# Keeping both halves of the spread conditioning vectors in SBUF, with Silu taken once on a DRAM copy

## The chip, the cores and the metric

One core of one Trainium2 chip runs the whole program. The metric is the device time of one execution in microseconds (us); lower is better. The engines are PE (TensorE), DVE (VectorE), ACT (ScalarE), POOL (GpSimd) and SP, which in this kernel issues every DMA. Each engine works through its own list of instructions strictly in order.

## The reference, cut to what matters

Two layers of a diffusion backbone on 256 latent and 256 context tokens, width 2048, everything in float32.

```python
sc, sc_ctx = silu(c), silu(c_ctx)                        # two vectors of 2048
for l in range(2):
    shift, scale, gate = split(sc @ w_ada[l] + b_ada[l], 3)
    shift_c, scale_c, gate_c = split(sc_ctx @ w_ada[l] + b_ada[l], 3)
    h_lat = rms_norm(x, norm_g[l]) * (1 + scale) + shift
    h_ctx = rms_norm(xc, norm_g[l]) * (1 + scale_c) + shift_c
    # projections of h by w_in[l]; attention of two kinds of heads; SiLU gates -> y
    x  = x + gate * (y_lat @ w_out[l])
    if l == 0:
        xc = xc + gate_c * (y_ctx @ w_out[l])
return rms_norm(x, final_g)
```

The products with `w_ada` are matrix times vector: 2 x 2048 x 6144 weights, for one or two vectors.

## The kernel before, in words

**Matmuls.** Every large product is done in three passes of a split: `wtile` (L105) loads a 512 KB tile of weights (`raw`, four slots, or at the start also `rad`, two slots), ACT copies it to `hi` (L114), DVE or, for each fifth tile, POOL forms `lo = raw - hi` (L116), and `mm3` (L138) issues three matmuls (L141 to L143). Results go to four PSUM banks `acc`, which DVE or ACT must empty (`evac_into`, L453 to L457) before PE can reuse them.

**Conditioning.** The shift and scale of layer 0 come from PE at the start (`ada_pe`, loads `ra`, L210, matmuls L229). The rest, gate of layer 0, shift, scale and gate of layer 1, is a background task (`ada_rest`, L296; one step of it is pulled in by `wtile` at a rate set by `bg_rate`). A step of `ada_half` (L252) loads a 512 KB tile `rad` of the transposed weights and lets DVE multiply and sum it with a half of `c`, spread over all partitions in the tile `cb` (L273, output `junk`, sum in `as`). With two vectors a step has four such instructions, here called **junk** instructions; there are 448 in all, on 128 `rad` tiles. `rad` has two slots, so a load waits until the junk instructions of the tile before last are done.

**The tile `cb`.** One slot (L250). Its first user is not the background task but the accumulator `q0` of the first query projection (L875), which holds it until the start of the first attention. `ada_rest` then goes through half 0, 1, 1, 0, 0, 1 of the vectors, and each call of `ada_half` takes a new `cb`, loads 1 MB into it by a broadcast DMA from DRAM (L259) and has ACT take Silu in place (L260). That makes six loads, six Silus and the changes between ACT's function tables that they bring, as attention uses Exp.

**Order.** A scheduler (`schedule_with_timeline_sim`) sets the order of each engine's list when the program is built, with the program's order as priority. So a change in what waits for what can move instructions far from the edit.

Layer 0 runs: first projections in seven parts while `w_ada` streams in (0 to 200 us); the last part of the projections `kv`, `q0`, `g0`, `q1` (`rest`, L925); attention of the first head group, for two blocks of heads (`gqa_heads`); projections `cq`, `ckv`, gates; the second group of heads (`mla_pair`, `mla_heads`); the output projection (`out_steps`, L773). Layer 1 follows in the same way.

## Time and profile before

| | us |
|---|---|
| median of three runs | 1416.0 (1414.63 to 1416.56) |
| the profiled execution | 1413.77 |
| its span (first to last instruction) | 1412.0 |
| PE busy | 1331.6 (94%) |
| DVE busy | 1094.0 (77%) |
| ACT busy | 602.6 (43%) |
| POOL busy | 404.0 (29%) |
| mean granted clock of PE | 0.984 of full speed |

The profile is one execution. Busy time is the sum of an engine's instructions; a view by stretches tells for each stretch how long each engine was busy, the clock that PE was granted (1.00 is 2.4 GHz, 0.50 is 1.2 GHz, and between them a mix of the two levels) and the share of the DMA engines in use. A row of waits names who waited for whom, with the total, the count and the longest. A row of the timeline has the start, the duration, the engine, the line, the operation, output<-input, and in brackets how long the engine was idle before it and what ended the wait.

### The profile page before, as it was taken

Reading aid. Unit: us, or ns where it says so; the run is one execution under the profiler, and the core shown is the slowest. Engines: PE = TensorE matmul, PEld = TensorE weight load, DVE = VectorE, ACT = ScalarE, POOL = GpSimd, SP = SyncE. Lnnn points to the kernel's source line nnn. Section 1 sums busy time; section 2 is a strip of 40 time slices with the busy share of each in tenths; the row PEclk is TensorE's granted clock in tenths of the full one; section 3 lists DMA queues with packets and bytes.
Section 4 is the critical chain, followed back from the end, with each engine's and each line's share of the span. In section 5 each row is a group of like instructions: output and inputs, shape, how many; then the busy total and the mean of one; then the engine's idle time right before and its main releaser. Section 6 shows DMA issues by size and latency. Waiting matters only on the chain.

```text
span 1412.0 us, 21026 instructions
## 1 busy us (share of the span) xinstructions
PE 1331.6 (94%) x7516; PEld 1128.1 (80%) x7516; DVE 1094.0 (77%) x2297; ACT 602.6 (43%) x974; POOL 404.0 (29%) x385
## 2 busy tenths in 40 slices
PE   5999999999997999898998999999999999999996
PEld 4776787877786987787886778898898989888884
DVE  2776548998887998989998965976787776857566
ACT  4322224535443242455532134665555644454443
POOL 0110015423223130221222213533234431223335
PEclk9999999999999999999999999999999999999999
DMA  9987733455554766443576665655775757733444
GB/s 310 354 276 268 271 104 104 135 164 181 160 187 155 209 217 199 148 147 120 179 247 210 209 214 178 202 161 169 237 257 162 237 156 259 257 108 124 157 139 144
DMA packets 142120, 272.47 MB, mean 193 GB/s; under 512 B 8336, under 2 KB 53824, under 8 KB 140608
## 3 DMA queue, kind: packets, MB, share of 16 engines
q1 hardware_dynamic: 142016, 271.13, 59.5%
q8 instruction: 59, 0.97, 0.3%
q14 instruction: 45, 0.37, 0.1%
HBM read 264.78 MB, written 6.32 MB: 192 GB/s over the span
## 4 chain that ended last, share of the span: by engine, by line
PE 55%; DVE 21%; DMA 11%; issue 6%; ACT 3%; POOL 2%; SPq 1%; DVEq 0%; POOLq 0%; ACTq 0%
PE acc L143 16%; PE acc L141 16%; PE acc L142 15%; DVE junk L273 8%; DMA rad<-in_w_adaT 7%; DVE lo L116 5%; PE att L592 3%; PE att L229 2%; PE att L615 1%; DMA raw<-in_w_in 1%; DMA cb<-in_cr 1%; DVE sm L597 1%; DVE pt L148 1%; DMA ra<-in_w_ada 1%; ACT hi L114 1%
## 5 line engine op out<-in xcount | busy, mean ns | idle before, releaser
L114 ACT CAST hi<-raw 128x1024 fp32r<-128x1024 f32 (+2 forms) x279 | 271.9, 977 | 380.1 <-PE acc L142 206.4
L116 DVE TENSOR_TENSOR lo<-raw,hi 128x512 fp32r<-128x512 f32 (+2 forms) x446 | 307.5, 731 | 88.8 <-PE acc L143 39.5
L116 POOL TENSOR_TENSOR lo<-raw,hi 128x512 fp32r<-128x512 f32 (+2 forms) x112 | 153.4, 1390 | 466.1 <-PE acc L143 317.4
L141 PE MATMUL acc<-hi,h 128*128 128x512 f32 (+1 forms) x672 | 239.3, 359 | 7.4 <-ACT cq L455 4.8
L142 PE MATMUL acc<-hi,h 128*128 128x512 f32 (+1 forms) x672 | 237.7, 356 | 0.0
L273 DVE CUSTOM_DVE_ANT_0 junk<-rad,cb 128x512 bf16<-128x512 f32 x224 | 175.0, 781 | 76.0 <-DMA rad<-in_w_adaT 50.4
L143 PE MATMUL acc<-lo,h 128*128 128x512 f32 (+1 forms) x672 | 227.4, 359 | 2.7 <-DVE lo L116 2.4
L273 DVE CUSTOM_DVE_ANT_0 junk<-rad,cb,as 128x512 bf16<-128x512 f32 x224 | 193.1, 862 | 3.8
L142 PE MATMUL acc<-h,lo 128*128 128x512 f32 (+1 forms) x512 | 171.4, 340 | 2.5 <-DVE lo L116 2.5
L143 PE MATMUL acc<-h,hi 128*128 128x512 f32 (+1 forms) x512 | 170.0, 338 | 0.0
L603 POOL TENSOR_SCALAR p<-p,sm 128x512 f32<-128x512 f32 (+1 forms) x96 | 85.8, 900 | 283.9 <-DVE sm L601 247.9
L141 PE MATMUL acc<-h,hi 128*128 128x512 f32 (+1 forms) x512 | 165.0, 341 | 0.3 <-ACT q L455 0.3
L143 PE MATMUL acc<-lo,y 128*128 128x512 f32 x384 | 146.3, 400 | 9.2 <-DVE lo L116 8.1
L141 PE MATMUL acc<-hi,y 128*128 128x512 f32 x384 | 150.7, 398 | 2.4 <-ACT y L147 2.0
L142 PE MATMUL acc<-hi,y 128*128 128x512 f32 x384 | 151.9, 396 | 0.2 <-DVE y L148 0.2
L141 PEld LDWEIGHTS acc<-hi,h 128*128 128x128 f32 x672 | 127.2, 189 | 28.9 <-ACT cq L455 5.0
L143 PEld LDWEIGHTS acc<-lo,h 128*128 128x128 f32 x672 | 124.6, 189 | 22.3 <-DVE lo L116 4.1
L142 PEld LDWEIGHTS acc<-hi,h 128*128 128x128 f32 x672 | 127.0, 189 | 15.5
L142 PEld LDWEIGHTS acc<-h,lo 128*128 128x128 f32 x512 | 96.8, 190 | 12.8 <-DVE lo L116 3.6
L143 PEld LDWEIGHTS acc<-h,hi 128*128 128x128 f32 x512 | 96.7, 190 | 9.8
L141 PEld LDWEIGHTS acc<-h,hi 128*128 128x128 f32 x512 | 93.6, 190 | 13.0 <-issue 2.5
L143 PEld LDWEIGHTS acc<-lo,y 128*128 128x128 f32 x384 | 73.4, 192 | 28.0 <-DVE lo L116 12.2
(219 smaller groups left out, 2281.4 us busy)
## 6 DMA issues: line engine op xcount, KB each, us to landing
rad<-in_w_adaT SPq DMA_DIRECT2D x128, 512.0 KB, 4.5
raw<-in_w_in SPq DMA_DIRECT2D x125, 512.0 KB, 4.5
raw<-in_w_out SPq DMA_DIRECT2D x72, 512.0 KB, 4.0
ra<-in_w_ada SPq DMA_DIRECT2D x32, 1024.0 KB, 8.4
raw<-in_w_in SPq DMA_DIRECT2D x48, 288.0 KB, 3.1
raw<-in_w_ukv SPq DMA_DIRECT2D x16, 512.0 KB, 3.5
cb<-in_cr SPq DMA_DIRECT2D x6, 1024.0 KB, 7.2
raw<-in_w_uq SPq DMA_DIRECT2D x12, 512.0 KB, 3.7
```

What stands on the lines that cost most here:

```text
L114: nc.scalar.copy(h, t)
L116: e.tensor_tensor(out=lo[:, c], in0=t[:, c], in1=fr(h[:, c]), op=ALU.subtract)
L141: mm(out, lhsT=ah, rhs=bh, start=first, stop=False)
L142: mm(out, lhsT=al, rhs=bh, start=False, stop=False)
L143: return mm(out, lhsT=ah, rhs=bl, start=False, stop=last)
L148: self.nc.vector.tensor_tensor(out=lo, in0=src, in1=fr(hi), op=ALU.subtract)
L229: nc.tensor.matmul(ps[32 * g : 32 * g + 32, :], lhsT=self.scp[:, m + i, o : o + 32], rhs=rs[kind, m][:, i, :], start=run is runs[0] and j ...
L273: nc.vector.tensor_tensor_reduce(out=junk, in0=r[:, cs], in1=cb[:, v, cs], scale=1.0, scalar=o if i else 0.0, op0=ALU.mult, op1=ALU.add, a ...
L592: self.order = nc.tensor.matmul(banks[j], lhsT=q[:, qs], rhs=k[:, ks], start=i == 0, stop=i == len(score) - 1)
L597: nc.vector.tensor_reduce(out=nb[:, c], in_=v, axis=AX.X, op=ALU.max)
L603: nc.gpsimd.tensor_scalar(out=pr[j], in0=pr[j], scalar1=l[:, j : j + 1], scalar2=1.0, op0=ALU.mult, op1=ALU.mult)
L615: nc.tensor.transpose(b[:, k, j * P : (j + 1) * P], pr[j][:, (i + k) * P : (i + k + 1) * P], self.ident)
```

## The change

The broadcast source becomes a small DRAM tensor `sc_d`. A new function `spread_c`, called in `layer0` after the third part of the first projections, loads both vectors as 32 rows of 128 into a temporary tile, takes Silu of them on ACT, and writes them to `sc_d`. The tile `cb` gets two slots, and `ada_half` keeps the tile of each half in a dictionary: the first call with half 0 loads it, the first call with half 1 loads the other, and the four later calls use what is there. Silu on the spread tile is gone. The scratch for DMA descriptors is set to 2 KB when the program is created.

```diff
+    def spread_c(self):
+        nc = self.nc
+        cr = self.tmp("cr")[: 2 * KT, :P]
+        nc.sync.dma_start(out=cr, in_=self.a["cr"].rearrange("v (k p) -> (v k) p", p=P))
+        nc.scalar.activation(cr, cr, AF.Silu)
+        self.sc_d = self.dp.tile([2, D], F32, name="sc_d")
+        nc.sync.dma_start(out=self.sc_d.rearrange("v (k p) -> (v k) p", p=P), in_=cr)
...
     def cb_tile(self):
-        return self.tp.tile([P, 2, 1024], F32, tag="cb", name=self.nm("cb"), bufs=1)
+        return self.tp.tile([P, 2, 1024], F32, tag="cb", name=self.nm("cb"), bufs=2)
...
     def ada_half(self, half, work):
-        cb = self.cb_tile()
         hs = slice(half * 1024, half * 1024 + 1024)
-        with self.behind():
-            nc.sync.dma_start(out=cb, in_=self.a["cr"][:, hs].partition_broadcast(P))
-        nc.scalar.activation(cb, cb, AF.Silu)
+        if half not in self.cb:
+            self.cb[half] = self.cb_tile()
+            with self.behind():
+                nc.sync.dma_start(out=self.cb[half], in_=self.sc_d[:, hs].partition_broadcast(P))
+        cb = self.cb[half]
...
                 modulated(nxt)
+            if p[0] == 2:
+                self.spread_c()
         self.start = False
...
-    nc = bacc.Bacc("TRN2", target_bir_lowering=False, num_devices=1)
+    nc = bacc.Bacc("TRN2", target_bir_lowering=False, num_devices=1, dynamic_dma_scratch_size=2048)
```

The edit makes the changed file longer: its L283 is L273 of the kernel before, L463 is L453, L465 is L455, L219 is L210, L329 is L319.

The order of the lists changes at three places. The first is **SP's list in the first projections**, behind the loads of the third part. Before (`cs` is a table for the rotary positions, `ra` weights of `ada_pe`):

```order
L96 DMA raw_812<-in_w_in 128x2x512
L486 DMA cs_798<-in_rope 128x512
L210 DMA ra_820<-in_w_ada 128x8x256
L210 DMA ra_822<-in_w_ada 128x8x256
L210 DMA ra_840<-in_w_ada 128x8x256
L210 DMA ra_842<-in_w_ada 128x8x256
```

After:

```order
L96 DMA raw_817<-in_w_in 128x2x512
L178 DMA cr_798<-in_cr 32x128
L496 DMA cs_803<-in_rope 128x512
L181 DMA sc_d<-cr_798 32x128
L219 DMA ra_825<-in_w_ada 128x8x256
L219 DMA ra_827<-in_w_ada 128x8x256
L219 DMA ra_845<-in_w_ada 128x8x256
L219 DMA ra_847<-in_w_ada 128x8x256
```

Four loads of `ra` now stand behind a write that waits for ACT's Silu.

The second is **DVE's list where the background task begins**. Before, it begins in the first attention, behind the first softmax (`q_55` is the accumulator of `q1`):

```order
L598 SCALAR_TENSOR_TENSOR sm_2096<-sm_2096,scq_810 128x2
L273 ISA junk_1651,as_1647<-rad_1649,cb_1644 128x512
L273 ISA as_1647 128x1
L453 TENSOR_TENSOR q_55_354<-acc_2469,q_55_354 128x512
L453 TENSOR_TENSOR q_55_354<-acc_2476,q_55_354 128x512
```

After, it begins behind the modulation of the last part, among the evacuations of `q0` (named `cb_326`) and `q1`:

```order
L375 SCALAR_TENSOR_TENSOR h_1405<-xT_100,mod_87,h_1404 128x256 x8
L283 ISA junk_1655,as_1651<-rad_1653,cb_1649 128x512
L283 ISA as_1651 128x1
L463 TENSOR_TENSOR cb_326<-acc_1437,cb_326 128x512
...
L116 TENSOR_TENSOR lo_1577<-rad_1574,hi_1576 128x512 x2
L283 ISA junk_1700,as_1651<-rad_1698,cb_1649 128x512
L283 ISA as_1651 128x1
L463 TENSOR_TENSOR q_55_354<-acc_1507,q_55_354 128x512
L463 TENSOR_TENSOR q_55_354<-acc_1514,q_55_354 128x512
```

The background task has moved ahead by the whole end of the projections. Counted in the two lists, the junk instructions that stand ahead of four points on DVE are: the last `qT` of the second block of heads, 51 before and 96 after; the first `kn` of the second head group, 230 and 283; that group's last maximum (L597), 316 and 365; the twelfth product with the gate in the output projection (L810), 392 and 392. From there on the counts agree.

The third is **ACT's list at the projection `cq`**. Before:

```order
L114 CAST hi_4165<-raw_4163 128x576
L260 ACT_TABLE_LOAD
L260 ACTIVATE cb_3746<-cb_3746 128x2048
L319 ACTIVATE junk_4035,sm_4034<-cq_3682 128x512
L455 COPY cq_3682<-acc_3709 128x512
L319 ACTIVATE junk_4056,sm_4055<-cq_3682 128x512
```

After:

```order
L114 CAST hi_4165<-raw_4163 128x576
L465 COPY cq_3685<-acc_3712 128x512
L329 ACTIVATE junk_4035,sm_4034<-cq_3685 128x512
L329 ACTIVATE junk_4056,sm_4055<-cq_3685 128x512
L114 CAST hi_4216<-raw_4214 128x576
```

The Silu of `cb` and its table load no longer stand ahead of the evacuation of `cq`. Over the whole list of ACT the table loads fall from 22 to 14, and SP's list has two loads of `cb` in place of six.

## Rows read from the trace of the kernel before

**Rows 1.** Stretches by stage: us, busy time (count) by engine, PE clock, DMA share, GB/s

```profile
176.00:243.00 67.00, 65.49 (x300) 53.82 (x299) 44.65 (x78) 21.72 (x32) 25.80 (x30) 1.00 0.31 95
243.00:329.00 86.00, 80.56 (x416) 67.65 (x415) 81.67 (x195) 39.09 (x69) 34.24 (x32) 0.96 0.51 160
329.00:577.00 248.00, 230.50 (x1230) 198.22 (x1229) 217.53 (x530) 91.80 (x145) 60.14 (x58) 0.98 0.59 186
577.00:731.00 154.00, 147.35 (x876) 128.76 (x875) 142.70 (x350) 77.23 (x145) 33.83 (x37) 0.99 0.49 157
731.00:857.00 126.00, 117.54 (x504) 94.44 (x503) 100.24 (x213) 34.59 (x51) 30.53 (x22) 0.96 0.65 213
857.00:1234.00 377.00, 367.39 (x2292) 329.75 (x2291) 285.05 (x527) 200.19 (x304) 138.55 (x130) 1.00 0.66 210
```

**Rows 2.** Waits of the whole run, total us, count, longest

```profile
DVE junk L273 <- DMA rad<-in_w_adaT: 50.4, 39, 4.2
DVE junk L273 <- ACT cb L260: 23.4, 5, 7.9
```

**Rows 3.** DVE's waits from 329 to 577 us

```profile
DVE junk L273 <- ACT cb L260: 13.2, 2, 7.9
DVE junk L273 <- DMA rad<-in_w_adaT: 10.4, 12, 2.0
```

**Rows 4.** DVE's longest wait from 577 to 731 us

```profile
DVE junk L273 <- ACT cb L260: 4.2, 1, 4.2
```

**Rows 5.** Timeline of ACT, then of PE, at the third load of `cb`

```profile
444.19 1.28 ACT L260 ACT_TABLE_LOAD   x1 [7.68 <-DMA cb<-in_cr]
445.48 1.91 ACT L260 ACTIVATE cb<-cb 128x2048 f32<-128x2048 f32 x1
...
448.53 0.61 PE L141 MATMUL acc<-hi,h 128*128 128x288 f32 x1 [4.77 <-ACT cq L455]
```

**Rows 6.** Stretch around it

```profile
436.00:460.00 24.00, 17.54 (x91) 15.38 (x91) 15.43 (x34) 11.03 (x20) 11.26 (x12) 0.86 0.44 145
```

**Rows 7.** Timeline of SP in the first projections

```profile
58.52 0.65 SPq L486 DMA_DIRECT2D cs<-in_rope  x1
60.72 0.37 SPq L210 DMA_DIRECT2D ra<-in_w_ada  x1
...
71.79 3.38 SPq L96 DMA_DIRECT2D raw<-in_w_in  x1
```

**Rows 8.** DMA issues from 55 to 90 us: size, median us to landing

```profile
ra<-in_w_ada SPq DMA_DIRECT2D x6, 1024.0 KB, 10.2
cs<-in_rope SPq DMA_DIRECT2D x1, 256.0 KB, 10.4
```

**Rows 9.** Chain of waits, the matmuls that use those `ra`

```profile
82.03 1.86 PE att L229 x32
```

**Rows 10.** Junk instructions from 176 to 329 us: busy us, mean ns, idle before

```profile
L273 DVE CUSTOM_DVE_ANT_0 junk<-rad,cb,as 128x512 bf16<-128x512 f32 x25 | 22.3, 891 | 0.3
L273 DVE CUSTOM_DVE_ANT_0 junk<-rad,cb 128x512 bf16<-128x512 f32 x26 | 19.9, 765 | 0.7 <-DMA rad<-in_w_adaT 0.6
```

**Rows 11.** Timeline of POOL, then of DVE, near 430 us

```profile
430.68 3.46 POOL L116 TENSOR_TENSOR lo<-raw,hi 128x512 fp32r<-128x512 f32 x2 [24.47 <-PE acc L143]
...
430.61 0.69 DVE L273 CUSTOM_DVE_ANT_0 junk<-rad,cb 128x512 bf16<-128x512 f32 x1
431.22 0.09 DVE L273 DVE_READ_ACCUMULATOR2_ANT as<- 128x1 f32 x1
431.34 1.65 DVE L273 CUSTOM_DVE_ANT_0 junk<-rad,cb,as 128x512 bf16<-128x512 f32 x1
```

**Rows 12.** Timeline of DVE, then of SP, near 186 us

```profile
185.66 1.29 DVE L116 TENSOR_TENSOR lo<-rad,hi 128x512 fp32r<-128x512 f32 x2 [4.85 <-PE acc L143]
186.88 1.28 DVE L453 TENSOR_TENSOR q<-acc,q 128x512 f32<-128x512 f32 x2
...
187.02 0.34 SPq L96 DMA_DIRECT2D rad<-in_w_adaT  x1
```

More of the change, by code (lines that the diff above doesn't have):

```diff
@@ L61, in __init__ @@
         self.bg = []
-        self.sums, self.ada_l1 = {}, False
+        self.sums, self.ada_l1, self.cb = {}, False, {}
         self.bg_rate = 0.0
```

## The prediction

> **What bounds the kernel now.** I read the stretches by stage first [rows 1]. PE is busy in 92 to 98% of every stage, so PE's work is the floor and only its idle time and its clock can be won. What a stage loses is its width minus PE's busy time, plus its width times what the clock lacks to 1.00 (while the clock is at its lower level a matmul takes twice as long). From 176 to 857 us that is 39.6 us of idle (1.5, 5.4, 17.5, 6.7 and 8.5 in the order of the rows) and 15.0 us of clock (0, 3.4, 5.0, 1.5, 5.0).
>
> The reader should then look at DVE in the same rows. From 243 to 329 it is busy for 81.7 of 86 us, from 577 to 731 for 142.7 of 154. There DVE sets the pace: it splits the weights, serves the softmax and does the junk instructions, all in one list. From 176 to 243 it has 22.4 us to spare, later less.
>
> The waits of DVE say where its spare time goes: 50.4 us on tiles `rad` that have not landed and 23.4 us on a Silu of `cb` [rows 2]. The second is what the change removes. The timeline at the third load of `cb` shows how such a wait reaches PE [rows 5]: ACT waits 7.68 us for the DMA with its table load, then takes 1.28 and 1.91 us, and the evacuation of `cq` stands behind. PE waits 4.77 us for it. The stretch around it has 6.5 us of PE idle, and a clock of 0.86, which is 3.4 us more [rows 6].
>
> **The change part by part.** The sum is made against the profiled execution, 1413.77 us (span 1412.0), which lies 2.2 us under the median of the three runs; the difference is put on the median, 1416.0.
>
> *Start, +1 us.* SP's list gets two small DMAs. The load `cr` stands where `cs` is issued at 58.52 [rows 7]; by `cs`'s landing of 10.4 us [rows 8] it is there at 69. The Silu of 32x128 is some tenths of a microsecond, so `sc_d` goes out at about 69.3, and the four `ra` loads behind it, the first of which went out at 60.72, follow one by one. In the rows the next `raw` goes out at 71.79 [rows 7], and four issues of 0.37 us from 69.7 end at 71.2, so what is behind them is not late. The queue still works off its backlog in that time. The matmuls that use these tiles start at 82.03 [rows 9], and 69.7 + 10.2 us to landing [rows 8] is 80. I take +1. Below it is 0; above, if the backlog is gone before, the 9 us from 60.72 to 69.7 less 4 of slack, +5.
>
> *Less on ACT and SP, 0 by itself.* Four loads of 1 MB and six Silus (11.5 us at 1.91) and eight table loads (10.3 us at 1.28 [rows 5]) go. ACT is busy for a quarter to a half of each stage [rows 1], so only the places where something waits behind them count, and these are in the stages below.
>
> *The junk instructions move forward.* By the counts in the lists, 45 more stand before the end of the first block of heads (329 us). The later stages have 187 instead of 179 (to 577), 82 instead of 86 (to 731) and 27 instead of 76 (to 857). One costs (22.3 + 19.9)/51 = 0.83 us [rows 10] and 0.09 for the read of its sum [rows 11], together 0.92.
>
> *176 to 329 us, +18.* The 45 cost 41.3 us of DVE. DVE's idle time there is 22.4 + 4.3 = 26.7 us [rows 1]. The last `qT` stands behind all of them, and PE needs it for the next block of heads, so 14.6 us stick out. Moreover one junk instruction now stands right behind the split whose end frees the `rad` slot that its tile needs, and two evacuations of `q1` stand behind it. In the trace the split ends at 186.9, the evacuations start at 186.88 and the load goes out at 187.02 [rows 12]; now the evacuations wait for the landing, up to the 4.2 us of the longest such wait [rows 2]. I take 3 to 4 us for such waits: +18. Below: at 0.69 us, which is what a junk instruction takes when POOL is quiet, plus the 0.09 [rows 11], 35 us minus 26.7 is +8. Above: if the 11 extra tiles (45 junk instructions, four to a tile) each wait 1.29 us (50.4/39 [rows 2]), 14.6 + 14.2 = +29.
>
> Here the trace and a rule have to be set against each other. POOL's split from 430.68 on takes 3.46 us, and the junk instruction that starts at 431.34 takes 1.65 us where the one before it took 0.69 [rows 11]. The Trainium skill (SBUF — State Buffer, section "SBUF: two separate sides") says that DVE instructions with two SBUF inputs and GpSimd instructions that read SBUF lock each other out of a shared pair of ports for a whole instruction. By that rule the moved instructions keep the higher price, as POOL works beside them there too, 25.8 of 67 us; without it the stage would cost +8. The mean of the rows has the lock in it, and the trace agrees.
>
> *329 to 577 us, -9.* Two of the waits for Silu, 13.2 us of DVE, go [rows 3], and 8 more junk instructions cost 7.4 us. By DVE's account that is -6. By PE's account the stretch around the third load alone holds 6.5 + 3.4 us [rows 6]. I take -9; the waits for `rad`, 10.4 us, stay. Bounds: 0, if DVE is late for another reason, and -14.
>
> At the removed table loads the Trainium skill (ScalarE: Activation LUTs, section "What ACT_TABLE_LOAD costs") would give more: 1.28 us for the load and about 1.38 us for draining, at each switch. In the trace the load at 444.19 ends at 445.47 and the Silu starts at 445.48 [rows 5], so no draining is seen behind it. By the page the third load's stall would be some 1.4 us dearer and this term about -10; I go by the row.
>
> *577 to 731 us, -6.* The wait of 4.2 us [rows 4] and four junk instructions (3.7 us) go, 7.9 us of DVE; PE cannot win more than its 6.7 idle and 1.5 of clock. Bounds -3 and -8.
>
> *731 to 857 us, -11.* 49 junk instructions, 45 us, leave a stage in which DVE was busy for 100.2 of 126. DVE is then far from the bound, and most of PE's 8.5 idle and 5.0 of clock goes. Bounds -8 and -13.5.
>
> *Later, -1.* The lists agree on the junk instructions. Two loads of `cb` go; of the 23.4 us, after 13.2 and 4.2, at most 6.0 is elsewhere [rows 2 to 4], and PE's 9.6 us of idle in 377 [rows 1] has many small causes. Bounds 0 and -3.
>
> The sum is 1 + 18 - 9 - 6 - 11 - 1 = -8: **1408 us**. The change pays back at the output projection what it takes at the first block of heads, and gains the stalls on `cb` on top.
>
> **The rivals.** *The early gaps take it all.* For it: DVE idles for 22.4 us from 176 to 243, and a DVE that is far ahead might leave PE no stall until 857. Then the price is +8, and 329 to 857 gives back all, -14, -8 and -13.5: 1 + 8 - 14 - 8 - 13.5 - 1 = -27.5, 1388.5 us. Against it: DVE is saturated from 243 on, and the number of junk instructions per stage stays the same until 731.
>
> *The end on the other side: `rad` ahead of the evacuations.* DVE's list is strict. From 176 us on a junk instruction stands ahead of nearly every evacuation of `q0`, `q1`, `g0`, `kv`, and each of its tiles can only be requested when a slot is free, on a queue where `raw` loads wait for their own slots. If the 11 extra tiles each hold DVE for 2.0 us (the longest wait in 329 to 577 [rows 3]), that is 22 us: the stage costs +36 and the sum is +10, 1426 us. It decides from 12 us of such waits on. For it: 50.4 us of waits for `rad` in the whole run. Against it: only 0.6 us of them are in the saturated first block [rows 10].
>
> *Nothing to measure.* SP's write waits for ACT longer than I think, DMA runs dry and the start costs +5; the second stage gains only -5: 1 becomes 5 and -9 becomes -5, so the sum is 0, 1416 us. That the change doesn't do what it says is excluded by the lists: two loads of `cb`, one Silu.
>
> **How the numbers follow.** The forecast's own case has 0.45 (1401 to 1414), the gaps 0.16, the waits for `rad` 0.23, nothing to measure 0.16. About 0.2%, 2.8 us, is what a measurement can tell from no change. Faster by more: 0.45 less 0.04, and 0.16, is 0.57; same: 0.16 and 0.04, 0.20; slower 0.23. The range leaves out half of each outer case, about 0.2: 1394 to 1424. It covers the bounds of the first attention stage, +8 to +29 with the rest as summed, 1398 to 1419.
>
> **What would show it.** Right: 128 tiles `rad` as before, the first junk instruction near 176 us; no wait for `cb`; DVE busy for over 95% from 176 to about 345; the second block of heads begins some 18 us later than at 329; the output projection has under 2 us of PE idle, and the lead is regained by its end. Wrong: the second block starts on time (the gaps took it), DVE waits over 12 us for `rad` before it (slower), the matmuls of 82 us start after 85 (the start), or new idle time of PE from 577 to 857.

## The result and the profile after

The change took **1398.6 us** in the median of four runs (1396.1 to 1401.3), the kernel before 1415.3 beside it: 16.7 us less, ratio 0.987 with an interval of 0.984 to 0.989. Two more sets of runs of the change, on other chips, gave 0.989 (0.987 to 0.991) and 0.987 (0.985 to 0.989). The forecast was 8 us less, inside a range that held the result; the gain was twice as large.

The profiled execution took 1399.7 us. Its first rows, the engines' busy time, stand against the small table of before:

```profile
span 1397.9 us, 20991 instructions
PE 1331.9 (95%) x7516; PEld 1131.7 (81%) x7516; DVE 1078.2 (77%) x2297; ACT 581.2 (42%) x961; POOL 399.2 (29%) x385
```

PE is busy as long as before (1331.9 and 1331.6 us), so between these two executions the whole gain, 14.1 us of span, is idle time of PE. The waits of DVE, to be held against [rows 2]:

```profile
DVE junk L283 <- DMA rad<-in_w_adaT: 62.9, 36, 5.5
```

The profile has no row for `cb` any more: its 23.4 us are gone. The waits for `rad` rose from 50.4 to 62.9.

The next view has the stretches by stage, cut at the same instructions as in [rows 1], 176, 329, 577, 731 and 857 us there (us, busy time and count of PE, PEld, DVE, ACT, POOL, the clock, DMA share, GB/s). The first row is from the kernel before, cut closely at the end of the last modulation `h` and the start of the 13th maximum; the others are from the change:

```profile
175.64:329.20 153.56, 146.61 (x717) 121.92 (x716) 126.88 (x274) 61.01 (x101) 60.40 (x62) 0.98 0.42 131
```

```profile
177.06:340.70 163.64, 153.38 (x717) 127.06 (x716) 157.13 (x363) 56.87 (x98) 62.20 (x62) 0.94 0.50 159
340.70:579.10 238.40, 229.20 (x1240) 198.05 (x1239) 222.75 (x547) 84.93 (x143) 61.72 (x58) 0.99 0.60 188
579.10:725.20 146.10, 141.84 (x848) 124.75 (x846) 138.42 (x346) 71.61 (x141) 33.41 (x36) 0.99 0.47 152
725.20:840.00 114.80, 114.61 (x518) 94.64 (x517) 54.13 (x110) 32.00 (x49) 25.57 (x21) 1.00 0.52 174
840.00:1398.00 558.00, 533.33 (x3189) 470.98 (x3187) 396.12 (x726) 279.57 (x440) 199.03 (x184) 0.99 0.57 183
```

The reader should see three things. In the first block the same 717 matmuls take 10 us longer, part in idle time, part in a clock of 0.94. DVE was busy for 30 us more there and filled 20 us of idle time. And in the output projection (725 to 840) PE has 0.2 us of idle left (0.9 and 0.8 in the two other profiles of the change), at full clock, with DVE busy for 54 us where it had been for 100.

Single executions scatter by 1 to 3 us in a stage, so the table has the mean of two profiles of the old order of lists (before, and the first experiment below, whose lists are those of before) and of three of the change (widths from the starts of the instructions named, read in the timelines):

| stretch (to the start of) | forecast | before | change | measured |
|---|---|---|---|---|
| start (last modulation `h`) | +1 | 175.2, 176.5 | 176.7, 175.8, 175.4 | +0.1 |
| first block of heads (13th maximum) | +18 | 153.9, 154.3 | 164.1, 165.5, 165.0 | +10.8 |
| to the first `kn` | -9 | 247.9, 247.5 | 238.4, 237.6, 237.2 | -10.0 |
| second group of heads (48th maximum) | -6 | 154.0, 154.8 | 146.1, 144.9, 145.0 | -9.1 |
| output projection (12th product) | -11 | 125.4, 125.1 | 114.9, 114.4, 114.4 | -10.7 |
| the rest | -1 | 555.5, 558.5 | 557.9, 560.7, 556.6 | +1.4 |

The sum is -17.5, 9.5 us beyond the forecast's -8. Of that, 7.2 us come from the first block and 3.1 from the second group of heads; the other four terms together make up for 0.8.

### The profile page after: what moved, and what is told of

It is laid out like the page before. It is cut to its first block, busy times and chain, and to the rows that moved or that the text cites. A ratio compares the mean times of both kernels' runs of the same rounds, so it can differ in the third digit from the quotient of the medians.

```text
span 1397.9 us, 20991 instructions
## 1 busy us (share of the span) xinstructions
PE 1331.9 (95%) x7516; PEld 1131.7 (81%) x7516; DVE 1078.2 (77%) x2297; ACT 581.2 (42%) x961; POOL 399.2 (29%) x385
## 4 chain that ended last, share of the span: by engine, by line
PE 54%; DVE 25%; DMA 11%; issue 5%; ACT 2%; POOL 2%; SPq 1%; DVEq 0%; POOLq 0%; ACTq 0%
PE acc L141 15%; PE acc L142 15%; PE acc L143 15%; DVE junk L283 10%; DMA rad<-in_w_adaT 7%; DVE lo L116 5%; PE att L602 3%; PE att L238 2%; DMA raw<-in_w_in 1%; PE att L625 1%; DVE sm L607 1%; DVE pt L148 1%; DMA ra<-in_w_ada 1%; DMA y<-y_d 1%; SPq L219 1%
## 5 line engine op out<-in xcount | busy, mean ns | idle before, releaser
L116 POOL TENSOR_TENSOR lo<-raw,hi 128x512 fp32r<-128x512 f32 (+2 forms) x112 | 150.0, 1360 | 471.6 <-PE acc L143 260.6
L283 DVE CUSTOM_DVE_ANT_0 junk<-rad,cb 128x512 bf16<-128x512 f32 x224 | 172.7, 771 | 65.1 <-DMA rad<-in_w_adaT 62.9
L283 DVE CUSTOM_DVE_ANT_0 junk<-rad,cb,as 128x512 bf16<-128x512 f32 x224 | 189.9, 848 | 3.4
L141 PE MATMUL acc<-hi,y 128*128 128x512 f32 x384 | 149.5, 394 | 2.1 <-ACT y L147 2.1
L142 PE MATMUL acc<-hi,y 128*128 128x512 f32 x384 | 149.8, 391 | 0.2 <-DVE y L148 0.2
L142 PEld LDWEIGHTS acc<-hi,h 128*128 128x128 f32 x672 | 126.8, 189 | 15.6
```

The source lines that it names most:

```text
L116: e.tensor_tensor(out=lo[:, c], in0=t[:, c], in1=fr(h[:, c]), op=ALU.subtract)
L141: mm(out, lhsT=ah, rhs=bh, start=first, stop=False)
L142: mm(out, lhsT=al, rhs=bh, start=False, stop=False)
L283: nc.vector.tensor_tensor_reduce(out=junk, in0=r[:, cs], in1=cb[:, v, cs], scale=1.0, scalar=o if i else 0.0, op0=ALU.mult, op1=ALU.add, a ...
```

## The experiments

Ratios are to runs of the kernel before on the same chip; 0.1% is 1.4 us.

### The scratch alone

```diff
-    nc = bacc.Bacc("TRN2", target_bir_lowering=False, num_devices=1)
+    nc = bacc.Bacc("TRN2", target_bir_lowering=False, num_devices=1, dynamic_dma_scratch_size=2048)
```

> The kernel before with the descriptor scratch of 2 KB alone; no list changes. All theories: 1414 to 1417. The profile of the change is 1.4 us late in its first 50 us already, ahead of every edit; if the small scratch is the cause, this one shows it too, and 1.4 us more in all.

Measured: 1415.6 us, ratio 0.999 (0.998 to 1.001): nothing. Its profile has the last `h` at 176.5 us, that of before at 175.2, a third one of the change at 175.4. So the 1.4 us belonged to the execution, neither to the scratch nor to the change.

### Which part of the change gains what

**The change with the late start.** Half 0 shares its slot with `q0` again:

```diff
-    def cb_tile(self):
-        return self.tp.tile([P, 2, 1024], F32, tag="cb", name=self.nm("cb"), bufs=2)
+    def cb_tile(self, half=0):
+        return self.tp.tile([P, 2, 1024], F32, tag=f"cb{half}", name=self.nm("cb"), bufs=1)
...
-            self.cb[half] = self.cb_tile()
+            self.cb[half] = self.cb_tile(half)
```

> The change, but the tile of half 0 shares its slot with the accumulator q0 again, so the background task begins in the first attention as before; half 1 has a slot of its own, and both stay. In DVE's list 51 junk instructions stand ahead of the last qT (before 51, change 96), 240 ahead of the first kn (230, 283), 330 ahead of the last maximum (316, 365), 392 ahead of the twelfth go. Theory A (the waits for cb are the gain, the early start is even: +10 us in the first block of heads, -10.6 in the output projection): no loss in the first block, about -7 to 577 us, -5 to 731, -2 at the output projection: 1402 us, between 1398 and 1405. Theory B (the early start is the gain, because most of the moved instructions run in time that DVE had to spare, and the waits for cb only stood beside other waits): most of the gain is gone, 1409 to 1414.

Measured: 1406.5 us, 0.992 (0.991 to 0.994), between the two theories. Its stretches: first block 157.4 (+3.3), to the first `kn` 236.5 (-11.2), second group 153.3 (-1.1), output projection 122.5 (-2.8). The stretch to the first `kn` gains its 11 us without any early start. Most of the gain of the second group and of the output projection needs the early start: that work has been done before.

**One slot and six loads, Silu taken in the DRAM copy:**

```diff
-        return self.tp.tile([P, 2, 1024], F32, tag="cb", name=self.nm("cb"), bufs=2)
+        return self.tp.tile([P, 2, 1024], F32, tag="cb", name=self.nm("cb"), bufs=1)
...
-        if half not in self.cb:
-            self.cb[half] = self.cb_tile()
-            with self.behind():
-                nc.sync.dma_start(out=self.cb[half], in_=self.sc_d[:, hs].partition_broadcast(P))
-        cb = self.cb[half]
+        cb = self.cb_tile()
+        with self.behind():
+            nc.sync.dma_start(out=cb, in_=self.sc_d[:, hs].partition_broadcast(P))
```

> The change with one slot for cb and six loads, as before; each load is from the DRAM copy with Silu taken. So the Silu and its table loads are gone, the wait for the transfer stays, and the background task begins late. Theory A: a wait for cb was some 6.6 us in the mean, of which the table load and the Silu are 3.2 after the landing; half of what the waits cost comes back, some -7 us: 1405 to 1411. Theory B: 1412 to 1416. A third theory, C (it is ACT's Silu and table loads in front of evacuations that cost PE, and the transfers are hidden): 1398 to 1404.

Measured: 1410.7 us, 0.995 (0.993 to 0.997), as theory A had it. DVE still waits 19.0 us for `cb`, now for the transfer. Without the Silus and table loads some 7 us are gained all the same, with hardly a change in where the work is done (51, 234, 320 and 392 junk instructions ahead of the four points, before 51, 230, 316 and 392).

**The kernel before with two slots,** six loads and six Silus (and the small scratch, which makes room for the slot):

```diff
-        return self.tp.tile([P, 2, 1024], F32, tag="cb", name=self.nm("cb"), bufs=1)
+        return self.tp.tile([P, 2, 1024], F32, tag="cb", name=self.nm("cb"), bufs=2)
```

> The kernel before with two slots for cb (and the small scratch that makes room): six loads, six Silus and 22 table loads stay, the task begins early (92 junk instructions ahead of the last qT, 277 ahead of the first kn, 366 ahead of the last maximum), and each load can be made while the other half is in use. Theory A and B: the waits for cb go and the early start is there, so nearly all of the gain: 1398 to 1403, with DVE's waits for cb under 3 us in all. Theory C: the Silus and table loads still stand on ACT: 1407 to 1413.

Measured: 1414.5 us (1408.1 to 1420.5), 0.998 (0.996 to 1.000). Theories A and B fall here: early start and early loads give almost nothing while the six loads with their Silus are there. Theory C's 1407 to 1413 is missed too. The waits of the whole run, and the timeline of ACT at the sixth load:

```profile
ACT cb L260 <- DMA cb<-in_cr: 12.0, 5, 5.6
DVE junk L273 <- ACT cb L260: 10.3, 2, 6.8
```

```profile
1097.06 1.28 ACT L260 ACT_TABLE_LOAD   x1
1103.95 1.92 ACT L260 ACTIVATE cb<-cb 128x2048 f32<-128x2048 f32 x1 [5.61 <-DMA cb<-in_cr]
1105.77 1.05 ACT L147 CAST qT<-att 128x512 fp32r<-128x512 f32 x2
```

The second slot halves DVE's waits for `cb` (10.3 us, before 23.4) and leaves ACT 12.0 us of waits for the transfers (before 17.3 in all). At the sixth load the Silu is placed in ACT's list while the transfer is still under way: ACT stands for 5.6 us and a copy that the attention needs stands behind it. Yet PE hardly feels it. Around ACT's two longest waits, at the fifth and the sixth load, PE is busy for 15.0 of 15 and for 16.1 of 17 us, at full clock:

```profile
785.00:800.00 15.00, 15.00 (x67) 12.41 (x67) 3.96 (x8) 6.24 (x5) 2.31 (x2) 1.00 0.64 194
1095.00:1112.00 17.00, 16.07 (x127) 15.55 (x127) 10.46 (x23) 8.48 (x9) 3.56 (x3) 1.00 0.65 223
```

What this kernel loses to the change, it loses mostly elsewhere: the second group of heads takes 154.3 us (the change 145 to 146) and the stretch behind the output projection 564.3 (557 to 561). The second group has no load, Silu or wait for `cb` in this kernel; what differs there is the order of the lists, with 89 junk instructions in the stage instead of 82. So part of what the six loads cost goes through the order that the scheduler chose, and these rows do not show what the waits of ACT cost by themselves.

**Two slots, six loads from the DRAM copy** (the diff above for six loads, without its first change), run twice:

> The change with two slots, but six loads from the DRAM copy with Silu taken (96 junk instructions ahead of the last qT, 282 ahead of the first kn). Against the two-slot kernel with Silus it takes away only the Silus and table loads. Theory C: with no ACT instruction that waits for a landing, nearly all of the change's gain: 13 to 18 us below before. Theory E (the slot and the transfer of the reloads are what costs): 3 to 8 us below, with DVE's waits for cb over 6 us in all.

> The change with two slots and six loads once more, for a second execution with a profile: the first profiled one (1401.9) was the fastest of eleven, whose median was 1408.1. If a reload that lands late makes the others slower, this one shows a wait for cb on DVE in the stage that is longer; if they are slower without one, the waits for rad, behind which or ahead of which the reloads stand on the queue, are longer in all.

Measured: 1408.1 us (1401.9 to 1413.4), 0.994 (0.992 to 0.996), between C and E; the second profiled execution took 1405.3. Beside the kernel with two slots and Silus the absence of six Silus is worth some 5 us. Neither profile has a wait for `cb`, against theory E, but the waits for `rad` are 74.2 and 73.0 us where the change's three profiles have 62.9, 68.3 and 65.6. With four loads more on the same queue DVE waits longer for `rad`. That the rest of the 8 us to the change lies there was not tested.

**Two loads with Silu in place, no DRAM copy:**

```diff
-                nc.sync.dma_start(out=self.cb[half], in_=self.sc_d[:, hs].partition_broadcast(P))
+                nc.sync.dma_start(out=self.cb[half], in_=self.a["cr"][:, hs].partition_broadcast(P))
+            nc.scalar.activation(self.cb[half], self.cb[half], AF.Silu)
...
-            if p[0] == 2:
-                self.spread_c()
```

> The change without the DRAM copy: two loads of the raw vectors, each with Silu in place, both early (16 table loads in all, 92 junk instructions ahead of the last qT, 280 ahead of the first kn). The two-slot kernel with six Silus gained only 2.7 us. Theory C (ACT, strictly in order, waits for the landing of cb with its Silu, and everything behind it waits too; the late ones in the heads and in layer 1 cost most): four of the six are gone, so 12 to 16 us below before. Theory D (the early two stand in the first attention and the last projection and are as dear as the others): 6 to 10 us below. That the copy with Silu in DRAM is worth nothing by itself: within 2 us of the change.

**The change once more, on the same chip:**

> The change itself, once more, on the chip of the three that follow, and with a second profile. All theories: 16 to 19 us below the kernel before. The first block of heads ends 9 to 12 us later than before, the output projection has under 1 us of PE idle again. If layer 1 (from the twelfth go to the end) is again 2 us longer than before, that is the kernel; if not, it was the execution.

Measured: 1399.4 us without the copy, 0.989 (0.987 to 0.991), and 1400.1 for the change, 0.989 (0.987 to 0.991). The DRAM copy and its function add nothing that can be measured; two early Silus cost nothing that can be measured either, and theory D falls. What gains is that each half is loaded once: that takes away the late Silus and the late transfers together. Theory C's time is met, its mechanism is not shown: of the 15.6 us between the profiles of the two-slot kernel with six Silus and of this one, 8.8 lie in the second group of heads, where neither has a Silu of `cb`.

The parts, by ratios: the Silus and their table loads 7 us with one slot and 5 with two, the reloads 4 us with the late start and 7 to 10 with the early one, the early start 5 to 8 us where nothing is reloaded, and under 3 where it is.

### What makes the first block late

The forecast had said: 45 junk instructions more, what exceeds DVE's idle time sticks out. Then fewer of them must make the block shorter. Six kernels change how many there are.

**Rate 0.8 until the first attention is done:**

```diff
-BGS, BG0, BG1, BG3, BG2 = 5.0, 1.3, 1.1, 0.5, 0.4
+BGS, BGE, BG0, BG1, BG3, BG2 = 5.0, 0.8, 1.3, 1.1, 0.5, 0.4
...
-        self.bg_rate = BG0
+        self.bg_rate = BGE
         self.bg += [self.ada_rest()]
...
+        self.bg_rate = BG0
         gate(2)
```

> The change with the background task's rate at 0.8 instead of 1.3 until the first attention's two blocks are through: 80 junk instructions ahead of the last qT (change 96), 251 ahead of the first kn (283), 336 ahead of the last maximum (365), 386 ahead of the twelfth go (392). The account of DVE says that 20 us of its idle time before 341 us were filled free, and that each junk instruction beyond is 0.7 to 0.8 us: the first block then ends 0 to 4 us later than before instead of 10 to 12, the second stage is as short, the output projection with 50 instructions has 2 to 5 us of idle: 3 to 8 us below the change. The rival, that the first block is late because of waits for rad and a clock that falls, not for DVE's work: no shorter first block, and the change's time or up to 4 us more.

Measured: 1412.5 us, 0.997 (0.996 to 0.999). A clear miss for both readings: 12 us slower than the change, and the first block 168.3 us. In it DVE waits for `rad` as the second rival of the forecast had it; the timeline of DVE, then of SP:

```profile
188.15 0.69 DVE L283 CUSTOM_DVE_ANT_0 junk<-rad,cb 128x512 bf16<-128x512 f32 x1 [6.54 <-DMA rad<-in_w_adaT]
```

```profile
162.62 16.70 SPq L96 DMA_DIRECT2D raw<-in_w_in  x3
179.37 0.46 SPq L269 DMA_DIRECT2D cb<-sc_d  x1
179.94 0.41 SPq L96 DMA_DIRECT2D rad<-in_w_adaT  x1
```

The slower rate moved the first loads of the task behind three `raw` loads that wait for slots; in the change `cb` goes out at 165.1.

**Rate 0.4, and 0.8, in the second half of the block only** (the start as in the change):

```diff
         for c in range(2):
+            self.bg_rate = (BG0, 0.4)[c]
             qT = self.pairT("qT")
...
+        self.bg_rate = BG0
         gate(2)
```

> The change with the background rate at 0.4 from the second half of the first attention's projections to the end of that attention, 1.3 before and behind. The start is that of the change (39 junk instructions ahead of the first maximum, where the slower dial had 29 and waited 13 us for rad); 76 stand ahead of the last qT (96), 247 ahead of the first kn (283), 332 ahead of the last maximum (365), 386 ahead of the twelfth go (392). By DVE's account: the first block 0 to 3 us longer than before instead of 10 to 11; the stretch to the first kn as in the change or 5 us shorter; the output projection with 54 instructions 4 to 6 us dearer than with 27 (the runs with 50 to 62 lost 5 to 9): 3 to 8 us below the change, 1392 to 1397. If the slow dial's loss was not its waits for rad, but that later stages pay for what is left undone: 1402 to 1410.

> The same with the rate at 0.8 in the second half: 39, 92, 263 and 348 junk instructions ahead of the four points, 386 ahead of the twelfth go. By DVE's account the first block is 7 to 10 us longer than before, the output projection with 38 instructions loses 1 to 4 us, and the stretch to 731 us is as in the change: 1396 to 1401. By the other reading 1400 to 1406.

Measured: 1413.7 us, 0.998 (0.997 to 0.999), and 1408.6, 0.994 (0.992 to 0.996): "the other reading", and more than it said. With 0.4 the block took 164.1 us, as in the change, though DVE had less work in its second half:

```profile
266.00:340.00 74.00, 64.88 (x334) 54.42 (x333) 62.10 (x152) 29.71 (x58) 27.81 (x30) 0.91 0.42 139
```

DVE is busy for 62 of 74 us, PE idles for 9 and has a clock of 0.91. But DVE's 12 idle us are no free time. The largest wait in them is again for `rad`, here under 1 us in the change:

```profile
DVE junk L283 <- DMA rad<-in_w_adaT: 7.5, 4, 2.9
```

So most of the time that the fewer instructions left free went to waits for their tiles. The 20 instructions left undone are paid for later: 242.1 us to the first `kn` instead of 238, 147.7 in the second group instead of 145, 120.8 in the output projection instead of 115.

**Half of the products of layer 0's gate left out,** those of the second vector:

```diff
             out = self.sums[l, kind][half]
+            if (l, kind) == (0, 2):
+                nc.gpsimd.memset(out, 0.0)
...
-                for v in vs:
+                for v in vs[: 1 if (l, kind) == (0, 2) else None]:
```

> The change, with the products of layer 0's gate left out for the second vector (64 of the 448 junk instructions; the tiles rad, their loads and the order's rates stay). 56 junk instructions stand ahead of the last qT instead of 96, on 28 tiles instead of 24. Read in the first block of heads alone. If its 10 to 11 us are DVE's work that did not fit in its idle time, 40 instructions fewer, at 0.67 to 0.79 us, take 27 to 32 us from DVE there and the block ends 0 to 2 us later than before. If they are waits for the tiles rad that stand ahead of evacuations, it still ends 7 us later or more, as the tiles are no fewer. The total time will be lower for the work that is left out and is no measure.

Measured in the block: 165.3 us, DVE busy for 130 of them, and 28.6 us of waits for `rad`. So the block is 11 us late with hardly more DVE work than before (127 us). That is no proof that DVE's work doesn't matter in the change, whose waits for `rad` in the block are 3 to 4 us: here the waits alone could make it late.

**The task begun behind `q0`, at two rates:**

```diff
-        self.bg += [self.ada_rest()]
...
             run(f"q{c}", rest, "add", lambda t: self.post_q(acc[f"q{c}"], c, t, qT))
+            if c == 0:
+                self.bg += [self.ada_rest()]
```

> The change, with the background task begun behind the last projection of q0 in the program instead of ahead of the last part of kv. In the lists 19 junk instructions stand ahead of the first maximum (change 39, before 0), 75 ahead of the last qT (96, 51), and PE has 32 more projection matmuls ahead of its first attention matmul than before, where the change has 74 more. Theory F (the early junk instructions delay q0's chain on DVE; the scheduler lets PE do projections meanwhile, and these are then missing between the heads, whose chain of maximum, Exp and scaling is too slow for PE alone): the first block is 3 to 6 us longer than before, not 10 to 13; later stages like the dial with 76 ahead of the last qT: stretch to 731 us 12 to 16 us shorter than before, output projection with 44 instructions 4 to 6 us dearer than the change: 1399 to 1404 in all. Theory G (an early beginning of the task costs 10 us in the first block, wherever it stands): 10 us longer, 1404 to 1410.

> The same with the rate at 2.0 instead of 1.3 until the third gate projection: 19, 76, 266 and 354 junk instructions ahead of the four points (change 39, 96, 283, 365), the same 32 projection matmuls. Theory F: the first block 3 to 6 us longer than before, the output projection with 38 instructions loses 1 to 4 us: 1395 to 1401. Theory G: 1402 to 1408.

Measured: 1412.5 us, 0.998 (0.996 to 1.000), and 1414.0, 0.999 (0.997 to 1.000). The block took 166.7 and 169.1 us. Theory F falls. G is nearer, with a block 13 and 15 us longer than before, but both totals lie above its range.

**More splits on POOL ahead of the first attention,** each second or each third tile instead of each fifth:

```diff
-        e = nc.gpsimd if POOL_LO and self.nlo % POOL_LO == 0 else nc.vector
+        e = nc.gpsimd if POOL_LO and self.nlo % self.pool_lo == 0 else nc.vector
...
         self.bg_rate = BG0
+        self.pool_lo = 2
...
+            self.pool_lo = POOL_LO
             self.gqa_heads(c, qT, gs[c], (0, 1))
```

> The change, with POOL taking each second tile's split instead of each fifth, from the last part of the projections to the first attention. The junk instructions stay where the change has them (38, 94, 283 and 365 ahead of the four points; change 39, 96, 283, 365), but DVE has fewer splits ahead of its first maximum, and PE has 31 projection matmuls more ahead of the attention than before instead of 74. Theory H (DVE is full before the first maximum, busy 83 of 88 us, so the heads begin 22 us late, and the block ends when their chain ends, long after the projections between them are used up): the heads begin 5 to 12 us earlier than in the change and the block ends 3 to 8 us earlier, all later stages as in the change: 1393 to 1398. Rival I (POOL's splits, 3.5 us a tile, are late for PE and block DVE's own instructions meanwhile): as much is lost before the first maximum as is gained, 1399 to 1406.

> The same with each third tile: 41, 97, 283 and 365 junk instructions, 70 projection matmuls more ahead of the attention than before. Theory H: the heads begin 2 to 5 us earlier, 1396 to 1400. Rival I: 1399 to 1404.

Measured: 1400.5 us, 0.988 (0.986 to 0.991), and 1395.6, 0.985 (0.983 to 0.988). With each second tile the heads begin 5 us earlier (first maximum at 260.5 instead of 265.4) and the block takes 170.3 us, longer, not shorter: theory H falls too, and the time is one that rival I had. With each third the block stays as it is, 164.9.

All kernels of this part, first block only. PE's loss is the width less its busy time, and what the clock lacks to 1.00 times the width:

| kernel | junk ahead of first maximum, of last `qT` | width | DVE busy | DVE's waits for `rad` | PE's loss |
|---|---|---|---|---|---|
| before | 0, 51 | 153.9 | 127 | 1 | 10 |
| change, late start | 0, 51 | 157.4 | 130 | 0 | 13 |
| change (three profiles) | 39, 96 | 164.1, 165.5, 165.0 | 157, 158, 158 | 3, 4, 3 | 20, 21, 20 |
| rate 0.8 | 29, 80 | 168.3 | 150 | 13 | 26 |
| rate 0.4, second half | 39, 76 | 164.1 | 146 | 11 | 22 |
| rate 0.8, second half | 39, 92 | 167.2 | 156 | 5 | 23 |
| products left out | 26, 56 | 165.3 | 130 | 29 | 20 |
| begun behind `q0` | 19, 75 | 166.7 | 146 | 6 | 20 |
| the same, faster | 19, 76 | 169.1 | 147 | 5 | 24 |
| POOL each second | 38, 94 | 170.3 | 159 | 4 | 26 |
| POOL each third | 41, 97 | 164.9 | 158 | 2 | 21 |

An early begin costs 10 to 16 us here beside the kernel before, 7 to 13 beside the one with the late start, and neither the number of junk instructions nor DVE's busy time orders the rows. That does not clear DVE. Where it works less it mostly waits longer for `rad`, in the same list; without these waits it idles for less than 5 us behind the first maximum in every row of the table. So the reading that DVE's list, work and waits together, sets the end of the block is left standing, and no kernel here separates it from the early begin as such.

On PE's side the loss is many short waits, and a clock that fell beside them. Before and behind the first maximum the change has:

```profile
177.06:265.40 88.34, 85.23 (x381) 69.92 (x380) 83.00 (x171) 26.55 (x39) 34.54 (x34) 0.98 0.46 142
265.40:340.70 75.30, 68.15 (x337) 57.14 (x336) 74.14 (x193) 30.32 (x59) 27.66 (x29) 0.89 0.56 180
```

That is a loss of some 5 us and some 15, where [rows 1] have 1.5 and 8.8: two thirds of the difference lie among the heads. One wait of the first part, DVE's timeline and then PE's:

```profile
236.75 1.10 DVE L283 CUSTOM_DVE_ANT_0 junk<-rad,cb 128x512 bf16<-128x512 f32 x1
237.78 0.08 DVE L283 DVE_READ_ACCUMULATOR2_ANT as<- 128x1 f32 x1
237.78 1.28 DVE L463 TENSOR_TENSOR g<-acc,g 128x512 f32<-128x512 f32 x2
```

```profile
238.60 0.48 PE L141 MATMUL acc<-hi,h 128*128 128x512 f32 x1 [2.43 <-DVE g L463]
```

The evacuation of `g0` stands behind a junk instruction; PE waits 2.4 us for the bank. Before, the same wait was 1.26. With fewer instructions in the block such waits are no shorter: from 305 us on PE waits 8.5 us in all with rate 0.4 (for the scaling on POOL, for `g`, for the copies `pt`), 7.2 in the change. Which order of the lists would avoid them was not found.

### The pair on one chip

> The kernel with each third split on POOL ahead of the first attention, now beside the change on one chip. Its first run was 1.5% below before, the change's two 1.3 and 1.1%. If the gain is real: 2 to 5 us below the change, in the same stages as in its first profile (layer 1 shorter by 1 to 4 us, the first block of heads as long). If it was the chip: within 1.5 us of the change.

> The change itself, for the comparison with e17_pool3: 1.1 to 1.3% below before. The first block of heads 10 to 12 us longer than before, layer 1 from the first maximum to the last 2 to 5 us longer, if these belong to the kernel.

Measured: 1396.2 us with more splits on POOL, 0.985 (0.982 to 0.987), and 1398.1 for the change, 0.987 (0.985 to 0.989). The intervals overlap: more splits on POOL are not shown to beat the change. Layer 1, from the first maximum to the last, took 301.3 us in this third profile of the change, after 302.5 and 305.4; the two of the old order had 299.9 and 301.1. Most of that difference is the execution's; a remainder of 1 or 2 us can't be told from it.

## Why the prediction was half right

Its mechanism stood: the waits for `cb` go, the first block of heads pays for work that the output projection is then rid of. The gain came out at twice the forecast because its largest term, the price in the first block, was too high, and the gain of the second group too low.

**Start, +1: right in size.** SP's write went out when the forecast said, but the four loads behind it were slower:

```profile
59.42 0.65 SPq L178 DMA_DIRECT2D cr<-in_cr  x1
60.13 0.41 SPq L496 DMA_DIRECT2D cs<-in_rope  x1
70.27 0.33 SPq L181 DMA_DIRECT2D sc_d<-cr  x1
70.69 5.78 SPq L219 DMA_DIRECT2D ra<-in_w_ada  x4
76.53 2.83 SPq L96 DMA_DIRECT2D raw<-in_w_in  x1
```

The next `raw` goes out 4.7 us later than in [rows 7], where the forecast had it on time. The backlog did not cover that. From 68 to 72 us the DMA was nearly dry, with a share of 0.16 (before 1.10, full):

```profile
68.00:72.00 4.00, 4.00 (x20) 3.36 (x21) 3.60 (x6) 1.64 (x3) 3.12 (x5) 1.00 0.16 48
```

PE was busy in all 4 of these us even so. The matmuls of 82.03 [rows 9] start at 82.1 to 83.4 in the change's three profiles, and the last `h` at 175.4 to 176.7, against 175.2 and 176.5. So the size was right though the queue ran empty, which the forecast had not expected.

**Less on ACT and SP, 0 by itself: not contradicted.** The kernel with six loads without Silu gains 7 us. In its profile the gains stand where the forecast had booked waits, 3.6 us in the stretch to the first `kn`, 1.6 in the second group and 4.4 in the output projection, and its first block is 3.7 longer. How much of that is ACT's work and how much DVE's waits behind it can't be told apart.

**176 to 329 us, +18: the step that failed,** measured +10.8. In "The 45 cost 41.3 us of DVE" the price is wrong. The forecast added up the recorded durations, 0.92 us for a junk instruction and its read, and held them against DVE's idle time. But records of DVE overlap, and busy time in all these views counts an overlap once: it is not the sum of the instructions, as the text ahead of the rows has it. The timeline of the change has one such pair:

```profile
183.03 0.68 DVE L283 CUSTOM_DVE_ANT_0 junk<-rad,cb 128x512 bf16<-128x512 f32 x1
183.64 0.08 DVE L283 DVE_READ_ACCUMULATOR2_ANT as<- 128x1 f32 x1
183.75 0.75 DVE L283 CUSTOM_DVE_ANT_0 junk<-rad,cb,as 128x512 bf16<-128x512 f32 x1
```

The next instruction starts 0.72 us after the first, which with its read has 0.76 in the records, and each neighbour takes part of the overlap. In the rows of the first block DVE's busy time rises by 157.13 - 126.88 = 30.3 us for 45 instructions, 0.67 each, not 41.3. Its idle time falls from 26.7 to 6.5 us. 30.3 - 20.2 is the 10.1 us of that execution, so the account closes; but it is only an account. Whether what does not fit in DVE's idle time is the reason stays open. With 20 instructions fewer, and 11 us of DVE's work less, the block was as long; 8 of the 11 us had become waits for `rad`. All early begins cost 10 to 16 us, and all keep DVE's list nearly full among the heads.

The Trainium skill (SBUF — State Buffer, section "SBUF: two separate sides") would have the moved instructions keep a dearer price wherever POOL works beside them. The trace agrees: in 177 to 341 us the two forms take 861 and 751 ns in the mean, as against 0.75 and 0.68 us in the pair above, beside which POOL does nothing.

```profile
L283 DVE CUSTOM_DVE_ANT_0 junk<-rad,cb,as 128x512 bf16<-128x512 f32 x48 | 41.3, 861 | 0.4
L283 DVE CUSTOM_DVE_ANT_0 junk<-rad,cb 128x512 bf16<-128x512 f32 x48 | 36.0, 751 | 3.2 <-DMA rad<-in_w_adaT 2.8
```

**Waits for `rad` ahead of the evacuations:** 3 to 4 us forecast, 2.8 in the second of these rows (4.1 and 3.2 in the two other profiles). As a rival (1426 us) it did not come about in the change, but the kernel with the slower rate shows that it exists: 13.0 us in the block, 6.5 of them at once. With the rate 0.4 and with products left out there are 10.7 and 28.6.

**329 to 577 us, -9: right,** -10.0. The place of the third load, a stretch as long as that of [rows 6], has now:

```profile
432.00:456.00 24.00, 21.92 (x114) 18.36 (x113) 23.09 (x53) 6.94 (x16) 9.10 (x9) 1.00 0.57 181
```

PE idles for 2.1 us instead of 6.5, at full clock; DVE has 0.9 us of idle left. The late-start kernel shows the same gain, so it does not come from the early start. By the Trainium skill (ScalarE: Activation LUTs, section "What ACT_TABLE_LOAD costs") this term would have been -10; executions differ by 1 us here, so the result does not decide between its 1.38 us of draining and [rows 5], which show none.

**577 to 731 us, -6: too small by 3,** beyond the bound of -8. That bound counted PE's idle time and clock of the stage alone. But the stretch now holds 848 matmuls instead of 876, and 19 of the 28 are of the output projection (14 in the two other profiles): they had filled gaps here and are done in the next stage, which has hardly any idle time with them.

**731 to 857 us, -11: right,** -10.7. The experiments give a scale for this term: PE idle in the stage with DVE's busy time, from the late start, the one with six loads, and the rate 0.8:

```profile
724.00:846.00 122.00, 114.49 (x504) 92.64 (x503) 83.85 (x179) 31.19 (x48) 27.74 (x20) 0.99 0.61 198
```

```profile
732.00:853.00 121.00, 114.52 (x502) 91.86 (x501) 95.78 (x205) 31.41 (x49) 31.89 (x21) 0.99 0.67 218
```

```profile
730.00:850.00 120.00, 114.56 (x512) 92.79 (x511) 74.40 (x155) 31.43 (x48) 27.41 (x21) 1.00 0.57 183
```

DVE at 54 us leaves PE 0.2 us of idle, at 74 some 5, at 84 and 96 some 7, at 100 some 8.5 (10.6 in the second profile of the old order). So the work is far from free long before DVE is full, and a forecast of this stage by counts works here. DVE's busy time is not all, though: the two-slot kernel with six Silus, at 54 us too, has 4.3 us of idle.

**Later, -1:** +1.4, within what executions differ by.

**The rivals.** The result lies below the 1401 us at which the forecast's own case ended, where it had "the early gaps take it all", 1388.5 us. The gaps did take most of it, at +10.8 instead of +8, but the stages behind gave -30 and not the -35.5 that it had. Of the signs named for being right, the second block of heads began 11.6 us later and not 18; the others held. The forecast's mistake was one of size, above all in the term that spoke against the change.

## What to carry to other kernels

A constant that is loaded and prepared again for each use should be loaded once, if there is room: here a second slot halved the waits for it and gained 0.2%, while loading once gained 1.1 to 1.3%. What such a wait costs is read at PE, in the same stretch: one wait of ACT for a transfer came with 6.5 us of PE idle around it, another, of 5.6 us, with 0.9. When work is moved into an engine's idle time, its price is the rise of that engine's busy time as a union of its records, not a sum of durations. And a smaller amount of moved work need not make a smaller delay: here a fifth fewer of the junk instructions in the block did not shorten it, as the engine waited longer for their tiles instead, and the later stages, with more left to do, took longer.

## What the runs showed that was not expected

Less work was slower: 64 of 448 junk instructions left out gave 1405.5 us in one run, beside 1398 to 1400 for the change. Its DVE waits 28.6 us for `rad` in the first block instead of 2.8, and 24.7 instead of 9.7 in the stretch to the first `kn`. The block is about as long as the change's; that stretch is 4 us longer. Whether these waits are the cause was not tested.

The granted clock made a third to a half of PE's loss in the first block of the change (6.8 to 10.2 of some 20 us). Towards its end, where PE waited six times for 0.4 to 1.0 us from 321 to 333 us, it was:

```profile
325.00:341.00 16.00, 13.29 (x59) 11.06 (x57) 15.78 (x41) 7.47 (x15) 7.04 (x10) 0.68 0.41 150
```

A clock of 0.68 is a mix of 2.4 and 1.2 GHz; over 16 us it lacks 5.1 us, more than the 2.7 us in which PE was idle.
